# One transformer layer on one core: a reordered entry with products that nothing reads, row sums with one product, and half of the last output projection in the banks of the scores

## The chip, the core and the metric

The kernel runs on one core of one Trainium2 chip. TensorE (PE) does the matrix products, VectorE (DVE), ScalarE (ACT) and GpSimd (POOL) the rest, and SyncE (SP) issues most of the DMAs. The metric is the device time in microseconds, the median over runs; before the change it is 1199.61 us (three runs, 1198.49 to 1199.99).

## The reference

One decoder layer on a sequence of 1024 tokens of width 1024, in float32: an entry LayerNorm, two groups of attention heads side by side (sliding window with sinks, and stick-breaking), one output projection over both, LayerNorm, SwiGLU, LayerNorm.

```
h = layer_norm(x, ln_in_g, ln_in_b)
proj = h @ w_in          # q, k, v of both groups
sb_out, swa_out = stick_breaking_attention(...), sliding_window_attention(...)
merged = concatenate([rms_norm(sb_out, sb_norm_g), rms_norm(swa_out, swa_norm_g)])
h = layer_norm(ALPHA * h + merged @ w_out, ln1_g, ln1_b)
h = layer_norm(ALPHA * h + (silu(h @ gate) * (h @ up)) @ w_down, ln2_g, ln2_b)
```

## The kernel before, in words

Float32 accuracy comes from splitting each operand into a high and a low part and adding three products (hi*hi, hi*lo, lo*hi, helper `mm3`, L169 to L175). A scheduler places the instructions of each engine in a fixed order; each engine then runs its own in that order, and a wait at one instruction holds all behind it. The stages, in order of time:

- **Entry (0 to about 50 us).** The gain and bias rows `g_in` and `b_in` are spread over the partitions by four products with a row of ones (L269) and copied by ACT (L270). The eight token tiles x0 to x7 are normed (`entry`, L303 to L314): statistics on DVE (L141), the power of the variance on POOL (L135), the scaling on DVE alone for x0 and x1 (L151, L154) and on ACT, DVE and POOL for the others (L161, L162, L164). PE turns each tile in two groups of four transposes (L117) in the banks `tr`; ACT takes the high part (`xh`, L121), PE subtracts it with the negated identity `negi` (L124), and ACT takes the low part (`xl`, L125). The normed tile goes to `h_dram` on ACT's queue. Weight strips (`w_sw`, 512 KB each) arrive in two buffers `raw`; ACT casts the high part (L108), POOL subtracts (L109).
- **Projections and attention (to about 490 us).** `xmul` makes k, v and q of a strip (24 products of 256 columns per chunk of 256 tokens, bank `pp`). For v the result is copied from PSUM by DVE (`vr`, L343) and turned by PE (`pv`, L346). Scores lie in the banks `z`, transposed weights in `tra` or `trp`, outputs in `av`. A helper (`merge`) interleaves the attention of one head pair with the projection of the next; in the last pair it interleaves the output projection of the window group (`c1_steps`).
- **Output projection** (`out_load`, `out_proj`, L505 to L535): once in `c1_steps` for the window group (adds to h, result to `acc_dram`), once after the attention for the stick-breaking group, in the order of chunks 0, 2, 1, 3. `out_load` brings a chunk `m` of 512 features by 256 tokens, splits it (L510, L511) and squares it in place (L512). `out_proj` makes the row sum of squares of a token tile with four products against ones (`pr`, L522), then two halves of 512 columns (`pc`, twelve products each); DVE scales and adds each half to `acc` (L533). `pr` and both `pc` lie in the two buffers of bank `pp`. After the second one each tile is normed, written to `h1_dram` and turned for the FFN (`put_b`, banks `tr` and `av`).
- **FFN (from about 556 us).** Gate and up by a scheme with seven products of half size, then the down projection and the last norm. The change does not touch it.

Of the kernel before, what the change touches and what calls it, by code (L numbers as in the profile page):

```python
# [21 lines left out]
P = 128  # L22
# [27 lines left out]
class Ordered:  # L50
# [13 lines left out]
    def matmul(self, *a, **k):  # L64
        self._queue(self.eng.matmul(*a, **k))

    def transpose(self, *a, **k):
        self._queue(self.eng.transpose(*a, **k))

    def dma_start(self, *a, **k):  # L70
        self._queue(self.eng.dma_start(*a, **k))
# [3 lines left out]
def layer(ctx: ExitStack, tc: tile.TileContext, x, ln_in, w_sw, w_sb, norm_g,  # L75
          sinks, rel_bias, onehot, w_out, ln1, w_gu, w_down, ln2, out):
    nc = tc.nc
    pe, act, dve, pool = nc.tensor, nc.scalar, nc.vector, nc.gpsimd
# [28 lines left out]
    def split_w(raw, hi, lo):  # L107
        act.copy(hi, raw)  # L108
        pool.tensor_tensor(out=lo, in0=raw, in1=_f(hi), op=ALU.subtract)  # L109

# [26 lines left out]
    def ln_stats(xt, n=2, eps=LN_EPS):  # L137
        bst = st.tile([P, n, 6], F32, tag=f"bst{n}", name="bst")
        w = D // n
        for i in range(n):  # L140
            dve.bn_stats(out=bst[:, i, :], in_=xt[:, i * w:(i + 1) * w])  # L141
        mv = st.tile([P, 2], F32, tag="mv", name="mv")
        dve.bn_aggr(out=mv, in_=bst)  # L143
        rstd = st.tile([P, 1], F32, tag="rstd", name="rstd")
        rpow(rstd, mv[:, 1:2], 1.0, eps)
        return mv[:, 0:1], rstd

    def ln_apply(dst, xt, g, b, fast=False, eps=LN_EPS):
        mu, rstd = ln_stats(xt, 2, eps)
        if fast:  # L150
            dve.scalar_tensor_tensor(out=dst, in0=xt, scalar=mu, in1=g, op0=ALU.subtract, op1=ALU.mult)  # L151
            for i in range(2):
                h = slice(i * 512, i * 512 + 512)
                dve.scalar_tensor_tensor(out=dst[:, h], in0=dst[:, h], scalar=rstd, in1=b[:, h],  # L154
                                         op0=ALU.mult, op1=ALU.add)
            return
        nmu = st.tile([P, 1], F32, tag="nmu", name="nmu")
        dve.tensor_scalar(out=nmu, in0=mu, scalar1=-1.0, scalar2=None, op0=ALU.mult)
        for i in range(2):
            h = slice(i * 512, i * 512 + 512)  # L160
# [40 lines left out]
    def strip(i, ahead=2):  # L201
        while len(loaded) < min(len(strips), i + ahead):
# [3 lines left out]
            split_w(raw, hi, lo)  # L206
# [59 lines left out]
    for i, dst in enumerate((g_in, b_in)):  # L266
        for h in (slice(0, 512), slice(512, D)):
            ps = bps.tile([P, 512], F32, tag=("pp", "av")[i], name="bc")
            pe.matmul(ps, row1, rows[i][:, h], start=True, stop=True)  # L269
            act.copy(dst[:, h], ps)  # L270
# [32 lines left out]
    def entry(t):  # L303
        xt = xts.pop(t)
        ln_apply(xt, xt, g_in, b_in, t < 2)
# [8 lines left out]
        act.dma_start(h_dram[t], xt)  # L314
# [24 lines left out]
    def put_v(ps, c0, nc_, vts):  # L339
# [3 lines left out]
        dve.tensor_copy(vr.rearrange("p a b -> p (a b)"), ps)  # L343
# [161 lines left out]
    def out_load(g, c):  # L505
# [7 lines left out]
        return mh, ml, m  # L513

    def out_proj(c, m, wo, acc):
        mh, ml, ss = m
        for i in range(2):
# [3 lines left out]
            for k in range(4):  # L521
                pe.matmul(pr, ss[:, k, tok], ones, start=(k == 0), stop=(k == 3))  # L522
# [6 lines left out]
            for d in range(2):  # L529
                ds = slice(d * 512, d * 512 + 512)  # L530
                ps = bps.tile([P, 512], F32, tag="pp", name="pc")
# [22 lines left out]
    entry(0)  # L554
    entry(1)
    for c in range(4):
# [4 lines left out]
        if c < 3:  # L561
            entry(2 * c + 2)
            entry(2 * c + 3)
        swa_q(0, 0, q0, c, 1)
        swa_q(0, 1, q0, c, 1)
        if c > 0:
            next(att0)
            next(att0)
# [28 lines left out]

    def c1_steps():
        ms = [out_load(1, 0), out_load(1, 1)]
        for c in range(4):  # L600
# [3 lines left out]
            if c < 2:  # L604
                ms.append(out_load(1, c + 2))

# [40 lines left out]
    ms = {c: out_load(0, c) for c in order[:2]}  # L647
    hs = {}
    d0, d1 = slice(0, 512), slice(512, D)
    for n, c in enumerate(order):  # L650
        if n in (1, 2):
            ms[order[n + 1]] = out_load(0, order[n + 1])
        for t, h in out_proj(c, ms[c], wo, load_acc(c, acc_dram)):
# [215 lines left out]
    with tc.tile_pool(name="dn", bufs=4, reuse_waits="tile") as dn:  # L869
# [8 lines left out]
        def one(t):  # L878
# [6 lines left out]
            mu, rstd = ln_stats(h[t], 4)  # L885
# [104 lines left out]
```

## Time and profile before

| | |
|---|---|
| median of three runs | 1199.61 us |
| the profiled execution: its own time, its span | 1199.59 us, 1197.9 us |
| mean granted TensorE clock | 0.986 |
| busy share PE, DVE, ACT, POOL | 96%, 70%, 49%, 49% |
| stretches of 30 us in which PE is busy under 27 us | 0 to 60, 360 to 390, 450 to 480, 540 to 570, the end |

The span is the time from the first to the last instruction of the profiled execution; 1.7 us of its own time lie around it. PE is busy nearly always, so a reader looks at what PE is given to do, and at the stretches in which it waits or runs at the lower clock level.

### The profile page before, as it was taken

The page shows a single profiled execution, that of the slowest core. Times are in us where ns is not written, and L with a number is a line of the kernel's source. Part 1 is how long each engine was busy: PE and PEld are TensorE (multiplying, and loading weights), DVE is VectorE, ACT ScalarE, POOL GpSimd, SP SyncE. Part 2 cuts the span into 40 slices and gives each one's busy share as a digit, 9 for nine tenths or more (in the row PEclk, how much of TensorE's full clock was granted, in tenths as well). Part 3 has the DMA queues.
Part 4 walks back from the last instruction along what each step waited for, and adds up shares of the span by engine and source line. Part 5 has one row for each costly group of instructions (what it writes and reads, how often), then busy time and mean ns, then how long its engine had stood idle before and what let it go on. Part 6 is the DMA issues. An engine that isn't in the chain of part 4 may idle for free. (4 is left out here: it accounts for less than half of the span.)

```text
span 1197.9 us, 17900 instructions
## 1 busy us (share of the span) xinstructions
PE 1154.2 (96%) x6394; PEld 997.9 (83%) x6394; DVE 837.7 (70%) x1291; ACT 581.3 (49%) x1255; POOL 591.8 (49%) x572
## 2 busy tenths in 40 slices
PE   6899999999998998998999999999999999999997
PEld 4888998999998887876888888888888888888885
DVE  8776687887889895866765555564565448899735
ACT  5666577767677654346333232223233224456531
POOL 5623435566646463214777657665577521000584
PEclk9999999999999998999999999999999999999999
DMA  7403012110105525243333223422232339853431
GB/s 249 167 15 93 27 28 76 28 62 25 48 19 182 196 93 191 83 141 141 114 132 114 89 79 115 131 90 96 97 114 97 106 111 388 328 185 106 131 123 70
DMA packets 59913, 140.17 MB, mean 117 GB/s; under 512 B 7046, under 2 KB 18863, under 8 KB 59825
## 3 DMA queue, kind: packets, MB, share of 16 engines
q1 hardware_dynamic: 45264, 110.19, 28.6%
q10 hardware_dynamic: 14560, 28.85, 6.2%
q8 instruction: 50, 0.82, 0.3%
q14 instruction: 39, 0.31, 0.1%
HBM read 95.23 MB, written 41.17 MB: 114 GB/s over the span
## 5 line engine op out<-in xcount | busy, mean ns | idle before, releaser
L109 POOL TENSOR_TENSOR w<-s,w 128x512 fp32r<-128x512 f32 x88 | 124.0, 1412 | 121.4 <-ACT w L108 121.4
L174 PE MATMUL pp<-xh,whi 128*128 128x256 f32 x544 | 157.3, 290 | 1.4 <-DVE q L337 1.4
L174 PE MATMUL pp<-xh,wlo 128*128 128x256 f32 x544 | 157.0, 289 | 0.0
L174 PE MATMUL pp<-xl,whi 128*128 128x256 f32 x544 | 156.6, 288 | 0.0
L108 ACT CAST w<-s 128x512 fp32r<-128x512 f32 x88 | 54.6, 622 | 201.9 <-PE pgu L730 119.9
L803 PE MATMUL pd<-bhl,ahl 128*128 128x512 f32 x612 | 139.2, 389 | 0.0
L803 PEld LDWEIGHTS pd<-bhl,ahl 128*128 128x128 f32 x612 | 114.8, 188 | 24.2 <-DVE bhl L795 0.4
L762 DVE TENSOR_TENSOR t<-t,pgu 128x512 f32<-128x512 f32 x88 | 60.0, 682 | 98.7 <-PE pgu L730 95.6
L454 POOL TENSOR_TENSOR s<-s,s 128x127 f32<-128x127 f32 (+2 forms) x96 | 91.5, 956 | 51.8 <-DVE s L450 25.0
L174 PEld LDWEIGHTS pp<-xh,whi 128*128 128x128 f32 x544 | 105.5, 194 | 2.5 <-DVE q L337 1.7
L174 PEld LDWEIGHTS pp<-xl,whi 128*128 128x128 f32 x544 | 105.2, 193 | 1.5 <-ACT xl L125 0.3
L174 PEld LDWEIGHTS pp<-xh,wlo 128*128 128x128 f32 x544 | 105.2, 193 | 1.3
L795 POOL TENSOR_TENSOR ahl<-ar,ahl 128x512 fp32r<-128x512 f32 x12 | 16.2, 1353 | 134.8 <-ACT ahl L794 134.7
L450 DVE TENSOR_TENSOR_SCAN s<-s,brk 128x128 f32<-128x128 f32 (+1 forms) x64 | 69.4, 1089 | 12.0 <-ACT s L441 11.2
L794 ACT CAST ahl<-ar 128x512 fp32r<-128x512 f32 x63 | 39.1, 622 | 77.1 <-PE pd L803 50.2
L112 ACT CAST at<-tra 128x256 fp32r<-128x256 f32 (+1 forms) x160 | 55.2, 355 | 36.4 <-DVE at L113 19.0
L395 POOL TENSOR_TENSOR L<-L,rd 128x512 f32<-128x512 f32 (+1 forms) x32 | 30.9, 988 | 81.7 <-DVE rd L393 80.0
L109 POOL TENSOR_TENSOR w<-gr,w 128x512 fp32r<-128x512 f32 x44 | 62.2, 1424 | 8.1 <-ACT w L108 8.1
L113 DVE TENSOR_TENSOR at<-tra,at 128x256 fp32r<-128x256 f32 (+1 forms) x160 | 58.8, 382 | 8.8 <-ACT at L112 7.5
L730 PE MATMUL pgu<-B11h,w 128*128 128x512 f32 x176 | 59.1, 397 | 2.1 <-ACT w L108 1.5
L441 ACT ACTIVATE s<-z 128x128 f32<-128x128 f32 (+2 forms) x96 | 47.6, 498 | 23.9 <-PE z L440 15.7
L730 PE MATMUL pgu<-T4h,w 128*128 128x512 f32 x176 | 57.9, 390 | 0.4 <-DVE t L762 0.4
(234 smaller groups left out, 3315.6 us busy)
## 6 DMA issues: line engine op xcount, KB each, us to landing
ar<-a_dram SPq DMA_DIRECT2D x73, 256.0 KB, 3.1
a_dram<-act ACTq DMA_DIRECT2D x33, 512.0 KB, 2.6
gr<-in_w_gu SPq DMA_DIRECT2D x24, 512.0 KB, 3.4
ur<-in_w_gu SPq DMA_DIRECT2D x23, 512.0 KB, 3.5
bq<-in_w_down SPq DMA_DIRECT2D x44, 256.0 KB, 5.2
raw<-in_w_sb SPq DMA_DIRECT2D x12, 512.0 KB, 3.6
h_dram<-x ACTq DMA_DIRECT2D x8, 512.0 KB, 5.2
m<-o_dram SPq DMA_DIRECT2D x32, 128.0 KB, 2.8
```

What stands on the lines that cost most here:

```text
L108: act.copy(hi, raw)
L109: pool.tensor_tensor(out=lo, in0=raw, in1=_f(hi), op=ALU.subtract)
L112: act.copy(hi, ps)
L113: dve.tensor_tensor(out=lo, in0=ps, in1=_f(hi), op=ALU.subtract)
L174: pe.matmul(ps, a, b, start=(i == 0), stop=(i == n - 1))
L441: act.activation(s2[:, 0:w], ps, AF.Sigmoid, scale=-SCALE)
L450: dve.tensor_tensor_scan(s2[:, 0:w][:, ::-1], s2[:, 0:w][:, ::-1], brk[:, 512 - w:][:, ::-1] if last else zero.broadcast_to([P, w]), 1.0 i ...
L454: pool.tensor_tensor(out=s1[:, 0:m], in0=s1[:, 0:m], in1=s2[:, 1:m + 1], op=ALU.mult)
L730: pe.matmul(ps, a, b, start=(start and n == 0), stop=(stop and n == 11), skip_group_check=True)
L762: add = lambda out, x: dve.tensor_tensor(out=out, in0=x, in1=ps, op=ALU.add)
L794: act.copy(w[:, 0], src)
L803: pe.matmul(pd[t], x, y, start=(first and k == 0 and n == 0), stop=(end and k == KF - 1 and n == 2), skip_group_check=True)
```

## The change

Six edits. (1) `entry` is cut in two: `norm` (norming, store) and `turn_in` (transposes). The statistics of tile t come on DVE after the last step of tile t-1; x2 to x7 are normed before the q products of a chunk and turned after them; x0 and x1 are stored on SP's queue. (2) `warm` adds 3, 12 and 6 products of `negi` with itself before, between and after the transposes of x0 and x1, in a bank of the scores; nothing reads them. (3) The first two strips are split in halves, after the copies of `g_in` and `b_in` on ACT. (4) The copy `vr` moves from DVE to ACT, twelve times. (5) `out_load` adds the four blocks of squares on POOL (two additions, eight chunks), and `pr` is one product in place of four, for sixteen tiles. (6) The chunk 0 of the last projection is loaded and split during `c1_steps`, and the first half of a tile's `pc` lies in a bank of the scores (`z`) for three of four chunks.

```diff
@@ Ordered: every operation of an engine can be recorded; a wait-free order can be added
-    def matmul(self, *a, **k):
-        self._queue(self.eng.matmul(*a, **k))
-
-    def transpose(self, *a, **k):
-        self._queue(self.eng.transpose(*a, **k))
-
-    def dma_start(self, *a, **k):
-        self._queue(self.eng.dma_start(*a, **k))
+    def __getattr__(self, name):
+        f = getattr(self.eng, name)
+        if not self.on:
+            self.last = None
+            return f
+
+        def call(*a, **k):
+            self._queue(f(*a, **k))
+        return call
+
+    def after(self, ins, before):
+        self.tc.add_manual_dep(
+            ins.ins, before.ins.name,
+            mybir.DependencyInfo(mybir.DependencyClass.NoSync, mybir.DependencyReason.DATA),
+            reason="traced order")
...
-    pe, act, dve, pool = nc.tensor, nc.scalar, nc.vector, nc.gpsimd
+    pe, act, dve, pool = Ordered(tc, nc.tensor), nc.scalar, nc.vector, nc.gpsimd
...
@@ strip: the first two weight strips are split in halves, the first after the copies of g_in and b_in
-            split_w(raw, hi, lo)
+            for k in (slice(0, 4), slice(4, KT)) if i_ < 2 else (slice(0, KT),):
+                ins = split_w(raw[:, k], hi[:, k], lo[:, k])
+                if i_ == 0:
+                    pe.after(ins, copied)
...
-            act.copy(dst[:, h], ps)
+            copied = act.copy(dst[:, h], ps)
...
@@ entry(t) becomes norm(t) and turn_in(t)
-    def entry(t):
+    ended = []
+
+    def warm(n):
+
+        ps = bps.tile([P, P], F32, tag="z", bufs=ZB, name="warm")
+        for i in range(n):
+            pe.matmul(ps, negi, negi, start=True, stop=True)
+
+    def norm(t):
+        xt = xts[t]
+        first, last = ln_apply(xt, xt, g_in, b_in, t < 2)
+        if t > 0:
+            for ins in first:
+                pe.after(ins, ended[t - 1])
+        ended.append(last)
+        (act if t > 1 else sp).dma_start(h_dram[t], xt)
+
+    def turn_in(t):
         xt = xts.pop(t)
-        ln_apply(xt, xt, g_in, b_in, t < 2)
...
-        act.dma_start(h_dram[t], xt)
...
-        dve.tensor_copy(vr.rearrange("p a b -> p (a b)"), ps)
+        act.copy(vr.rearrange("p a b -> p (a b)"), ps)
...
@@ out_load, out_proj: squares summed on GpSimd, one product for the row sum, a bank per half
-        return mh, ml, m
-
-    def out_proj(c, m, wo, acc):
+        pool.tensor_tensor(out=m[:, 0:2], in0=m[:, 0:2], in1=m[:, 2:4], op=ALU.add)
+        pool.tensor_tensor(out=m[:, 0], in0=m[:, 0], in1=m[:, 1], op=ALU.add)
+        return mh, ml, m[:, 0]
+
+    def out_proj(c, m, wo, acc, banks=("pp", "pp")):
...
-            for k in range(4):
-                pe.matmul(pr, ss[:, k, tok], ones, start=(k == 0), stop=(k == 3))
+            pe.matmul(pr, ss[:, tok], ones, start=True, stop=True)
...
-                ps = bps.tile([P, 512], F32, tag="pp", name="pc")
+                ps = bps.tile([P, 512], F32, tag=banks[d], name="pc")
...
-    entry(0)
-    entry(1)
+    norm(0)
+    norm(1)
+    pe.on, pe.last = True, None
+    warm(3)
+    turn_in(0)
+    warm(12)
+    turn_in(1)
+    warm(6)
+    pe.on = False
...
-        if c < 3:
-            entry(2 * c + 2)
-            entry(2 * c + 3)
+        for t in (2 * c + 2, 2 * c + 3)[:NT - 2 - 2 * c]:
+            norm(t)
         swa_q(0, 0, q0, c, 1)
         swa_q(0, 1, q0, c, 1)
+        for t in (2 * c + 2, 2 * c + 3)[:NT - 2 - 2 * c]:
+            turn_in(t)
...
@@ c1_steps and the last projection
             if c < 2:
                 ms.append(out_load(1, c + 2))
+            elif c == 2:
+                m0.append(out_load(0, 0))
...
-    ms = {c: out_load(0, c) for c in order[:2]}
+    ms = {0: m0[0], order[1]: out_load(0, order[1])}
...
-        for t, h in out_proj(c, ms[c], wo, load_acc(c, acc_dram)):
+        for t, h in out_proj(c, ms[c], wo, load_acc(c, acc_dram), ("z" if n < 3 else "pp", "pp")):
```

The helpers `ln_stats`, `ln_apply` and `split_w` return the instructions that `after` is called with.

The scheduler's order on ACT at the entry, after the table load; before the change (`whi` and `whu` are the high parts of weight strips, `x_158` and `x_163` are x0 and x1, `x_199` and `x_201` x2 and x3, `xh_134` and `xl_135` hold x0 and x1):

```order
L270 COPY g_in<-bc 128x512 x2
L270 COPY b_in<-bc 128x512
L108 CAST whi<-raw 128x1024 x2
L270 COPY b_in<-bc 128x512
L121 CAST xh_134<-trx 128x4x128
L125 CAST xl_135<-trx 128x4x128
L314 DMA h_dram_84<-x_158 128x1024
L121 CAST xh_134<-trx 128x4x128
L314 DMA h_dram_85<-x_163 128x1024
L121 CAST xh_134<-trx 128x4x128
L108 CAST whi<-raw 128x1024
L161 ACTIVATE x_199<-x_199,nmu 128x512 x2
```

After the change (x0 to x3 are `x_158`, `x_163`, `x_203`, `x_205`):

```order
L282 COPY g_in<-bc 128x512 x2
L282 COPY b_in<-bc 128x512 x2
L115 CAST whi<-raw 128x512 x4
L129 CAST xh_134<-trx 128x4x128 x2
L133 CAST xl_135<-trx 128x4x128 x2
L115 CAST whi<-raw 128x1024
L303 COPY es<-pe__233 8x384
L115 CAST whu<-raw 128x1024
L304 DMA e_dram<-es 8x384
L129 CAST xh_134<-trx 128x4x128
L169 ACTIVATE x_203<-x_203,nmu 128x512 x2
L129 CAST xh_134<-trx 128x4x128
```

The second half of `b_in` now comes ahead of the casts of the first strips, the two stores are gone from ACT, and the casts of the third and fourth strip (`whi` 128x1024, `whu`) stand ahead of the high part of x1.

The scheduler's order on PE at the start of the last projection (`wo` is the weight of the window group, `woh` and `wol` that of the stick-breaking group); before the change:

```order
L174 MATMUL pc<-wo_5317,whi 128x512 x2
L174 MATMUL pc<-wo_5317,wlo 128x512
L487 MATMUL av<-at,v 128x256
L488 MATMUL av<-at,v 128x256
L487 MATMUL av<-at,v 128x256
L488 MATMUL av<-at,v 128x256
L522 MATMUL pr<-ones,m 128x1 x4
L174 MATMUL pc<-woh,whi 128x512
L174 MATMUL pc<-wol,whi 128x512
L174 MATMUL pc<-woh,wlo 128x512
L174 MATMUL pc<-woh,whi 128x512
```

After the change:

```order
L183 MATMUL pc<-wo_5345,whi 128x512 x2
L183 MATMUL pc<-wo_5345,wlo 128x512
L550 MATMUL pr<-ones,m 128x1
L514 MATMUL av<-at,v 128x256
L466 MATMUL z<-kd,q 128x512
L467 MATMUL z<-kl,q 128x512
L515 MATMUL av<-at,v 128x256
L514 MATMUL av<-at,v 128x256
L515 MATMUL av<-at,v 128x256
L183 MATMUL pc<-woh,whi 128x512
L183 MATMUL pc<-wol,whi 128x512
L183 MATMUL pc<-woh,wlo 128x512
```

The first twelve products of the last projection stood behind the last output products of their stretch and behind `pr`; now they follow the last scores (`z`) directly, with the last token tile of the window group and the last transposes and outputs of the attention still to come, and their `pr` comes later.

## Rows read from the trace of the kernel before

**Rows 1.** The page's first part: busy us, share and instructions by engine.

```profile
PE 1154.2 (96%) x6394; PEld 997.9 (83%) x6394; DVE 837.7 (70%) x1291; ACT 581.3 (49%) x1255; POOL 591.8 (49%) x572
```

**Rows 2.** PE's waits: us in total, times, longest.

```profile
PE pv L346 <- DVE vr L343: 4.8, 4, 1.9
...
PE pr L522 <- DVE res L533: 2.7, 1, 2.7
...
PE av L487 <- ACT at L112: 1.5, 1, 1.5
...
PE pr L522 <- ACT m L512: 1.1, 1, 1.1
PE av L488 <- DMA res<-acc_dram: 0.9, 1, 0.9
```

**Rows 3.** Windows: length, busy us by engine, granted clock, DMA share, GB/s.

```profile
80.00:90.00 10.00, 8.05 (x51) 7.33 (x50) 6.92 (x14) 6.02 (x16) 3.51 (x4) 0.83 0.05 16
195.00:200.00 5.00, 4.77 (x28) 4.77 (x29) 2.99 (x7) 4.36 (x11) 3.90 (x7) 0.66 0.55 159
380.00:395.00 15.00, 12.26 (x64) 10.66 (x65) 13.58 (x22) 12.12 (x24) 5.99 (x7) 0.77 0.69 226
465.00:480.00 15.00, 11.46 (x48) 9.26 (x47) 7.34 (x13) 7.79 (x14) 1.91 (x2) 0.77 0.56 200
520.00:525.00 5.00, 5.00 (x20) 4.05 (x19) 4.52 (x9) 1.26 (x2) 1.83 (x2) 0.66 0.29 109
420.00:460.00 40.00, 40.00 (x233) 34.73 (x233) 35.19 (x55) 22.11 (x52) 27.88 (x36) 1.00 0.30 102
```

**Rows 4.** Timeline of PE in the entry: start, us, instruction, idle before.

```profile
17.73 1.97 PE L117 MATMUL trx<-ident,x 128*128 128x128 f32 x8 [4.01 <-DVE x L154]
...
24.15 0.56 PE L174 MATMUL pp<-xl,whi 128*128 128x256 f32 x1
24.51 0.41 PE L174 MATMUL pp<-xh,wlo 128*128 128x256 f32 x1
24.72 0.41 PE L174 MATMUL pp<-xh,whi 128*128 128x256 f32 x1
...
47.69 0.39 PE L174 MATMUL pp<-xh,whi 128*128 128x256 f32 x1 [1.44 <-DVE q L337]
...
48.04 0.28 PE L174 MATMUL pp<-xh,wlo 128*128 128x256 f32 x1
48.15 0.28 PE L174 MATMUL pp<-xh,whi 128*128 128x256 f32 x1
```

**Rows 5.** Timeline of PE around a row sum.

```profile
381.81 0.95 PE L522 MATMUL pr<-ones,m 128*128 128x1 f32 x8
382.62 0.37 PE L487 MATMUL av<-at,v 128*128 128x256 f32 x1
```

**Rows 6.** POOL's groups from 370 to 480 us: busy, mean ns, idle before.

```profile
L454 POOL TENSOR_TENSOR s<-s,s 128x511 f32<-128x511 f32 x5 | 5.5, 1091 | 0.4
```

**Rows 7.** Timeline of DVE in the entry.

```profile
8.93 1.27 DVE L151 SCALAR_TENSOR_TENSOR x<-x,mv,g_in 128x1024 f32<-128x1024 f32 x1
...
11.07 3.32 DVE L151 SCALAR_TENSOR_TENSOR x<-x,mv,g_in 128x1024 f32<-128x1024 f32 x1
```

**Rows 8.** Timeline of POOL in the entry.

```profile
10.54 2.76 POOL L109 TENSOR_TENSOR wlo<-raw,whi 128x1024 fp32r<-128x1024 f32 x1 [2.10 <-ACT whi L108]
...
43.52 6.04 POOL L164 TENSOR_TENSOR x<-x,b_in 128x512 f32<-128x512 f32 x4
```

**Rows 9.** Timeline of ACT at the end of the attention.

```profile
465.76 1.04 ACT L510 CAST whi<-m 128x1024 fp32r<-128x1024 f32 x1 [6.22 <-DMA m<-o_dram]
466.71 0.36 ACT L112 CAST at<-tra 128x256 fp32r<-128x256 f32 x1
```

**Rows 10.** Timeline of DVE in the last projection.

```profile
518.33 1.41 DVE L533 SCALAR_TENSOR_TENSOR res<-pc,r,res 128x512 f32<-128x512 f32 x2 [4.74 <-DMA res<-acc_dram]
```

**Rows 11.** Timeline of ACT in the entry.

```profile
11.59 0.58 ACT L270 COPY b_in<-bc 128x512 f32<-128x512 f32 x1
```

**Rows 12.** The tile raw in the first 60 us: DMA times.

```profile
DMA to landing us min/median/max: 3.6/5.0/6.8
```

More of the change, by code (lines that the diff above doesn't have):

```diff
@@ L107, in split_w @@
     def split_w(raw, hi, lo):
-        act.copy(hi, raw)
+        ins = act.copy(hi, raw)
         pool.tensor_tensor(out=lo, in0=raw, in1=_f(hi), op=ALU.subtract)
+        return ins
     def split_ps(ps, hi, lo):
@@ L138, in ln_stats @@
         bst = st.tile([P, n, 6], F32, tag=f"bst{n}", name="bst")
-        w = D // n
+        w, first = D // n, []
         for i in range(n):
-            dve.bn_stats(out=bst[:, i, :], in_=xt[:, i * w:(i + 1) * w])
+            first.append(dve.bn_stats(out=bst[:, i, :], in_=xt[:, i * w:(i + 1) * w]))
         mv = st.tile([P, 2], F32, tag="mv", name="mv")
@@ L145, in ln_stats @@
         rpow(rstd, mv[:, 1:2], 1.0, eps)
-        return mv[:, 0:1], rstd
+        return mv[:, 0:1], rstd, first
     def ln_apply(dst, xt, g, b, fast=False, eps=LN_EPS):
-        mu, rstd = ln_stats(xt, 2, eps)
+        mu, rstd, first = ln_stats(xt, 2, eps)
         if fast:
@@ L153, in ln_apply @@
                 h = slice(i * 512, i * 512 + 512)
-                dve.scalar_tensor_tensor(out=dst[:, h], in0=dst[:, h], scalar=rstd, in1=b[:, h],
-                                         op0=ALU.mult, op1=ALU.add)
-            return
+                last = dve.scalar_tensor_tensor(out=dst[:, h], in0=dst[:, h], scalar=rstd, in1=b[:, h],
+                                                op0=ALU.mult, op1=ALU.add)
+            return first, last
         nmu = st.tile([P, 1], F32, tag="nmu", name="nmu")
-        dve.tensor_scalar(out=nmu, in0=mu, scalar1=-1.0, scalar2=None, op0=ALU.mult)
+        last = dve.tensor_scalar(out=nmu, in0=mu, scalar1=-1.0, scalar2=None, op0=ALU.mult)
         for i in range(2):
@@ L164, in ln_apply @@
             pool.tensor_tensor(out=dst[:, h], in0=dst[:, h], in1=b[:, h], op=ALU.add)
+        return first, last
     def bc_load(dst, src):
@@ L596, in load_acc @@
         return res
+    m0 = []
     def c1_steps():
@@ L884, in one @@
                 return
-            mu, rstd = ln_stats(h[t], 4)
+            mu, rstd, _ = ln_stats(h[t], 4)
             for x in (d0, d1):
```

## The prediction, made before the changed kernel was run

> **What bounds the kernel now.** I read the page's busy shares first [rows 1]: PE is busy 1154.2 of 1197.9 us, so 44 us are idle, and next to nothing can be won on another engine alone. The list of PE's waits comes second [rows 2]: the reader is to see that no wait dominates; the longest sums are 4.8 us for the copy `vr` and 2.7 us before a row sum, and three waits of 0.9 to 1.5 us stand together at the end of the attention. Third come windows with the granted clock [rows 3], because a wait costs twice: after it PE works for some microseconds at the lower level. In 465 to 480 PE is idle 15 - 11.46 = 3.5 us, and a clock of 0.77 costs another 0.23 x 15 = 3.45 us; in 380 to 395 the two are 2.7 and 3.45 us, in 195 to 200 1.7 us of clock, in 520 to 525 1.7 us, in 80 to 90 1.95 and 1.7 us. The middle of the attention is the contrast: from 420 to 460 PE is busy all the time at clock 1.00, and there a product left out is time won.
>
> The entry must be read from the timeline [rows 4], since its clock column says 1.00 although the products tell otherwise: at 24.5 us a product of 256 columns follows the last after 0.21 us (256 / 0.21 is 1.2 GHz), at 48 us after 0.11 to 0.12 us (2.4 GHz). PE had waited 4.01 us for x0's second half just before.
>
> **The change part by part.** All sums are made against the profiled execution's own 1199.59 us; the median of the runs, 1199.61, is the same for this purpose.
>
> *Row sums.* Four products against ones are eight instructions here, and the next product on PE starts 382.62 - 381.81 = 0.81 us after the first [rows 5]. One product leaves two of the eight, 0.20 us. Sixteen tiles save 16 x 0.61 = 9.7 us of PE. Eight tiles lie in `c1_steps`, where PE is dense, and count fully; the other eight lie in the last projection, where DVE and DMAs also end waits, and I count 60% of their 4.9 us: -7.8 us. In place of the products POOL gets two additions for each of eight chunks, about 1.1 us by a row of the same width [rows 6] and half of that for the half as wide one, 8 x 1.65 = 13.2 us in all, and POOL is busy 27.9 of 40 us there [rows 3]. They are hidden unless `pr` is the next thing PE needs, or unless they hold DVE up. Bounds: -9.7, and +13.2 - 9.7 = +3.5 if every addition delayed DVE by its length and DVE set the end.
>
> On that last point a row speaks against the change. The scaling of x0 takes 1.27 us; that of x1, the same instruction, takes 3.32 us from 11.07 [rows 7], and meanwhile POOL works on a weight strip from 10.54 to 13.30 [rows 8]. The wait is 13.30 - 11.07 = 2.2 us, which is 3.32 less 1.27 to within 0.2. The Trainium skill, "SBUF — State Buffer", section "Who interferes with whom", says that a VectorE instruction with two SBUF inputs contends with a GpSimd instruction that reads SBUF, and that the later one blocks until the other is done. The trace agrees at this place; by that rule each added POOL addition can block DVE, which is the rival "lock" below.
>
> *Chunk 0 loaded early.* Before, ACT stands 6.22 us at the cast of `m`, and the cast of attention weights that PE needs is behind it [rows 9]. Those are the three waits of 1.5, 1.1 and 0.9 us, and the low clock from 470 on. Now the first chunk's load, cast and square lie among the attention's work, four loads and not eight are left at that place, and twelve products of the last projection fill PE there. The load of chunk 2 still needs the attention's third chunk, and its cast still stands ahead of the last attention casts. Bounds 0 and -(3.5 + 3.45) = -7; I take -5.
>
> *Half of `pc` in the scores' banks.* Before, `pr` waits 2.7 us for DVE, which itself waits 4.74 us for the load of `acc` [rows 10]. This load is late in both kernels, because SP's queue has four stores ahead of it that wait for finished norms. What changes is that PE can go on: with `pc` in `z` and `pp` the next `pr` and twelve products, 0.2 + 12 x 0.21 = 2.7 us, need no bank of DVE's. The wait of 2.7 us goes, and with it the 1.7 us of clock. Late next is the second half of that tile, in `pp`. Bounds 0 and -4.4; I take -3.
>
> *The copy `vr` on ACT.* It is a matter of the queue, not of the copy's length: before, the copy waits behind scans and additions, and four `pv` wait 4.8 us for it. ACT is less busy, but the copy now stands behind softmax exponentials and casts that wait themselves. Bounds: all of it gone with the clock it costs, -(4.8 + 1.7 + 3.45) = -9.95; or each of the eight wide ones stalls as the worst one does, 1.9 us, with a clock loss behind it of up to 3.45 us: 8 x 5.35 - 9.95 = +33. Nearer to the first, since the work in between on PE is about as long as before: -2.
>
> *Entry.* Both halves of `b_in` are copied before the weight casts, so its second half comes not at 11.59 but one cast of 1.05 sooner, at 10.6 [rows 11]; x0 is finished one step of 0.7 later (half of the 1.27 of [rows 7]), at about 11.3, and turned 6 us earlier. x1 isn't: its variance power on POOL now comes behind four half strips, 4 x 1.3 us (half of 2.76 or a little less, [rows 8]) from 11.2, so x1 ends near 18 as before. Then ACT holds x1's high part back: ahead of it is the cast of the fourth strip, whose load is issued when POOL is done with the second (about 16.5) and lands 3.6 us later at best, 20.1, so the cast ends at 21.1 and x1's two high parts follow at 21.7 and about 23.6. The first low-part product comes at 24.8, not earlier than before (24.15) [rows 4]. What is won lies behind it: the q products of chunk 0 no longer stand behind transposes of tiles that POOL hasn't finished, and POOL's last entry addition ends at about 46, not 49.6 [rows 8], as it starts on x2 1.5 us sooner and the six tiles have less between them. By hand I get chunk 1's first product at about 43.4 against 47.69 us; 1.2 us of that is work moved behind it, so -3. Bounds: -8 when the wait and clock of 80 to 90 us (3.65) and more go as well, +3.2 when the strip's load takes 6.8 us and not 3.6 [rows 12]. The stores on SP put the later x loads at 18 us and not 17.5, which x5 to x7 can bear.
>
> *The products that nothing reads* are 21 of 128 columns, 0.1 us each at the low level: three ahead of the spreading of the gains (0.3 us), twelve in a wait for x1, six ahead of the low-part products (0.65 us, in the sum above). I count no gain for the clock: between the twelve and the first projection product PE still waits some 3 us for ACT.
>
> *The new order.* Nearly every row between 50 and 550 us moves a little. The old order has 4.8 + 2.7 + 1.5 + 1.1 + 0.9 = 11 us of such waits [rows 2]; that the new one makes or takes half as much in other places bounds the price by -5.5 and +5.5. I take half the upper end, +2.8.
>
> Sum: -7.8 - 5 - 3 - 2 - 3 + 2.8 = -18.0, so 1199.6 - 18.0 = 1181.6 us.
>
> **The rivals.**
> - *All waits go.* Row sums in full, chunk 0 and the banks at their bounds and the copy at half of its own: -9.7 - 7 - 4.4 - 5 - 3 = -29, 1170.5 us; if the clock also rises before chunk 0's k products, 24 x (0.21 - 0.12) = 2.2 us more, 1168. For it: these waits have one cause each. Against it: the fixed order of five engines changes with them.
> - *The freed time isn't on the path.* DVE is busy 35.2 of 40 us from 420 to 460 and the loads of `acc` come no earlier, so PE waits where it worked. Then the entry and half of the window group's share stay: 1199.6 - 3 - 2.5 = 1194. Against it: DVE waits for PE in the last projection more than the reverse.
> - *Lock.* The additions of POOL block DVE: of the 13.2 us what falls on a busy DVE is given back, 35.2 of 40 us in the one stretch and 7.3 of 15 in the other [rows 3], some 0.7 on the mean: 9.2 us, 1181.6 + 9.2 = 1191.
> - *Nothing that can be measured.* The new waits eat the gain: 1199.
> - *Slower: `vr` behind ACT's queue.* Place: the eight wide v copies between 120 and 385 us. Price: 1.9 us and 3.45 us of low clock each. With all eight, 1181.6 + 2 + 33 = 1217; it decides from the fifth stalled copy on, as the other terms hold 16 us and n copies cost n x 5.35 - 9.95. For it: the copy now shares a queue with casts that wait for DVE. Against it: PE's order has about as many other products directly ahead of `pv` as before.
>
> **How the numbers follow.** No change is what lies within 0.2%, 2.4 us, about what a measurement of this kernel can tell. Forecast (1174 to 1189) 0.58; all waits go 0.12; not on the path 0.14, one part in ten of it within 0.2%; lock 0.06; nothing 0.04; slower 0.06. Faster: 0.58 + 0.12 + 0.126 + 0.06 = 0.89; same 0.05; slower 0.06. The range goes from 1168 (the second clock level of the first rival) to 1197; some 0.05 lies below it and 0.11 above.
>
> **What would show it.** Row sums: `pr` with a quarter of the instructions and the dense stretch before 460 some 5 us shorter. Chunk 0: no wait of ACT for `m` over 3 us, and clock over 0.9 in the 15 us that answer to 465 to 480. Banks: no wait of PE over 1 us before a `pr`. Copy: `pv` waits under 4.8 us in all. Entry: chunk 1's first product before 45 us, POOL's last entry addition before 47. It is wrong if one of those stretches is as long as before, or if `pv` waits 10 us for ACT. From the gate products on, at 556 us, nothing should differ but a shift.

## The result and the profile after

The changed kernel takes 1191.0 us (median of 4 runs, 1188.7 to 1192.6) against 1199.8 before; the ratio is 0.992, 95% interval 0.9906 to 0.9935. So 8.8 us were won where 18.0 were forecast. The sign was right, the time lies in the range, but 2 us above the likeliest case's own range. The profiled execution took 1192.59 us (span 1190.8), the slowest of the four.

Where it came from, by a few events of PE's timeline, each from the one profiled execution of its kernel (start in us; the v transposes are the products `pv`, two at a time for each of chunks 0 to 3 at first, four at a time, "wide", from 180 us on):

| kernel | chunk 1's v | first wide v | last v | last pc | median, us | ratio to before |
|---|---|---|---|---|---|---|
| before | 55.6 | 183.1 | 381.3 | 543.9 | 1199.8 | |
| after | 61.7 | 189.2 | 384.5 | 536.0 | 1191.0 | 0.9906 to 0.9935 |
| e1 old entry, rest new | 55.8 | 179.6 | 374.3 | 533.5 | 1187.9 | 0.9877 to 0.9907 |
| e2 new entry alone | 61.9 | 188.5 | 388.0 | 550.5 | 1205.8 | 1.0032 to 1.0062 |
| e3 scalings held | 64.0 | 190.0 | 385.0 | 536.4 | 1193.7 | 0.9934 to 0.9958 |
| e4 vr on DVE | 61.6 | 187.9 | 387.2 | 543.7 | 1197.0 | 0.9971 to 0.9996 |
| e5 scalings held in two parts | 59.9 | 188.5 | 382.0 | 540.0 | 1195.4 | 0.9944 to 0.9972 |
| e6 four products | 61.6 | 189.0 | 384.2 | 539.9 | 1195.1 | 0.995 to 0.9975 |
| e7 chunk 0 late | 61.4 | 188.9 | 384.0 | 533.7 | 1192.4 | 0.9925 to 0.995 |
| e8 old entry, vr on DVE | 57.2 | 185.0 | 382.0 | 535.2 | 1191.2 | 0.9919 to 0.9944 |
| e9 fourth strip later | 56.0 | 187.5 | 383.2 | 534.3 | 1188.7 | 0.9879 to 0.9912 |
| e10 old first tiles | 57.4 | 182.9 | 378.1 | 529.9 | 1187.7 | 0.988 to 0.9908 |
| e11 one kind of bank | 60.6 | 187.7 | 382.9 | 544.3 | 1199.1 | 0.9983 to 1.0004 |
| e12 no unread products | 60.4 | 184.0 | 377.1 | 534.7 | 1190.0 | 0.9899 to 0.9926 |

PE's order differs between some of them, so that up to 2 us of work more or less lies ahead of an event. Between chunk 1's v and the first wide v the kernels take 123.6 (e12) to 131.5 us (e9), so what is won at the one does not arrive unchanged at the other. From the last v to the last `pc` the change takes 536.0 - 384.5 = 151.5 us and not 162.6: 11 us won. The entry loses 6.1 us by chunk 1's v. The attention in between takes 195.3 us and not 198.3. From the gate products on there is a shift, as forecast (548.61 to the span's end 642.2 us, before 641.1).

The page of the changed kernel, engines as in [rows 1], and its waits of PE, as in [rows 2]:

```profile
PE 1147.4 (96%) x6319; PEld 989.4 (83%) x6319; DVE 836.0 (70%) x1279; ACT 584.5 (49%) x1269; POOL 622.0 (52%) x590
```

```profile
PE trx L132 <- ACT xh L129: 4.7, 2, 4.3
...
PE pv L373 <- ACT vr L370: 1.9, 1, 1.9
...
PE pr L550 <- POOL m L541: 1.2, 1, 1.2
...
PE pr L550 <- DVE res L561: 0.2, 1, 0.2
```

Of the 4.8 us for `vr` 1.9 are left, and of the 2.7 us before a row sum 0.2; on top stands one wait of 4.3 us, and it is in the entry. Windows, as in [rows 3]: the first two are the entry, the last answers to the end of the attention.

```profile
30.00:40.00 10.00, 4.95 (x40) 4.32 (x38) 10.00 (x15) 2.79 (x6) 8.56 (x6) 0.82 0.33 135
40.00:47.00 7.00, 5.94 (x27) 5.71 (x28) 5.87 (x11) 4.79 (x12) 5.71 (x6) 0.53 0.44 169
465.00:480.00 15.00, 15.00 (x85) 12.95 (x84) 7.79 (x17) 6.04 (x13) 4.04 (x5) 1.00 0.77 277
```

The end of the attention is full at clock 1.00, where 11.46 us and 0.77 stood. The entry is the reverse: PE idles 5 of 10 us, then works at 0.53. Its chain is read backwards through four timelines of the changed kernel (start, us, instruction, idle before). PE, to set beside [rows 4]:

```profile
25.18 1.38 PE L71 MATMUL warm<-negi 128*128 128x128 f32 x6
26.35 0.52 PE L183 MATMUL pp<-xl,whi 128*128 128x256 f32 x1
...
41.06 0.80 PE L132 MATMUL trx<-xh,negi 128*128 128x512 f32 x1 [4.25 <-ACT xh L129]
...
41.89 0.41 PE L183 MATMUL pp<-xl,whi 128*128 128x256 f32 x1
42.10 0.41 PE L183 MATMUL pp<-xh,wlo 128*128 128x256 f32 x1
...
53.21 0.36 PE L183 MATMUL pp<-xh,whi 128*128 128x256 f32 x1
```

ACT, and under it DVE:

```profile
35.43 0.33 ACTq L330 DMA_DIRECT2D h_dram<-x  x1
35.80 0.37 ACT L370 COPY vr<-pp 128x256 f32<-128x256 f32 x1 [3.21 <-POOL x L172]
39.65 0.37 ACT L355 CAST kd<-pp 64x256 fp32r<-64x256 f32 x1 [3.48 <-DVE kl L357]
...
40.42 0.58 ACT L129 CAST xh<-trx 128x512 fp32r<-128x512 f32 x1
```

```profile
23.55 2.28 DVE L170 SCALAR_TENSOR_TENSOR x<-x,rstd,g_in 128x512 f32<-128x512 f32 x1 [0.80 <-ACT x L169]
...
25.88 0.69 DVE L170 SCALAR_TENSOR_TENSOR x<-x,rstd,g_in 128x512 f32<-128x512 f32 x1
...
29.98 1.28 DVE L149 BATCH_NORM_STATS2 bst<-x 128x6 f32<-128x512 f32 x2
31.18 6.44 DVE L170 SCALAR_TENSOR_TENSOR x<-x,rstd,g_in 128x512 f32<-128x512 f32 x5
...
37.66 1.62 DVE L170 SCALAR_TENSOR_TENSOR x<-x,rstd,g_in 128x512 f32<-128x512 f32 x1
39.21 0.41 DVE L357 TENSOR_TENSOR kl<-pp,kd 64x256 fp32r<-64x256 f32 x1
```

POOL, as in [rows 8]:

```profile
22.91 2.37 POOL L116 TENSOR_TENSOR wlu<-raw,whu 128x1024 fp32r<-128x1024 f32 x1
25.91 3.05 POOL L172 TENSOR_TENSOR x<-x,b_in 128x512 f32<-128x512 f32 x2 [0.63 <-DVE x L170]
28.92 1.06 POOL L143 TENSOR_TENSOR rstd<-mv,mhalf 128x1 f32<-128x1 f32 x2
...
31.99 8.42 POOL L172 TENSOR_TENSOR x<-x,b_in 128x512 f32<-128x512 f32 x5 [1.29 <-DVE x L170]
...
43.94 6.34 POOL L172 TENSOR_TENSOR x<-x,b_in 128x512 f32<-128x512 f32 x4 [1.29 <-DVE x L170]
```

PE waits for a high part that ACT casts at 40.42. ACT stood 3.48 us at the cast of the second head's k, because DVE had not done the first head's low part `kl`; that one stood behind six scalings in a row, 1.29 us each beside POOL's additions, where one alone takes 0.69. They began only at 31.2. Two things lie ahead of them. On POOL x3's power comes at 28.9, behind x2's additions, and these behind the fourth strip's subtraction `wlu`, which also holds up DVE's first scaling of x2. On DVE itself the scheduler has put the statistics of x4, x5 and x6 first, the last from 29.98, so DVE is busy until 31.2 and never stands still for the power. In the kernel before six scalings in all stand ahead of `kl` (x2 to x4; now eight, x2 to x5), and the last five run from 24.25, seven us sooner, under PE's k products, and `wlu` comes at 34. Its DVE and its POOL:

```profile
24.25 6.47 DVE L162 SCALAR_TENSOR_TENSOR x<-x,rstd,g_in 128x512 f32<-128x512 f32 x5
...
33.09 0.42 DVE L330 TENSOR_TENSOR kl<-pp,kd 64x256 fp32r<-64x256 f32 x1 [1.18 <-ACT kd L329]
```

```profile
25.36 4.80 POOL L164 TENSOR_TENSOR x<-x,b_in 128x512 f32<-128x512 f32 x3
34.32 2.36 POOL L109 TENSOR_TENSOR wlu<-raw,whu 128x1024 fp32r<-128x1024 f32 x1
```

### The profile page after: what moved, and what is told of

It reads as the page before. It is cut to its first block, busy times and chain, and to the rows that moved or that the text cites. A ratio compares the mean times of both kernels' runs of the same rounds, so it can differ in the third digit from the quotient of the medians.

```text
span 1190.8 us, 17761 instructions
## 1 busy us (share of the span) xinstructions
PE 1147.4 (96%) x6319; PEld 989.4 (83%) x6319; DVE 836.0 (70%) x1279; ACT 584.5 (49%) x1269; POOL 622.0 (52%) x590
## 5 line engine op out<-in xcount | busy, mean ns | idle before, releaser
L481 POOL TENSOR_TENSOR s<-s,s 128x127 f32<-128x127 f32 (+2 forms) x96 | 94.6, 990 | 42.6 <-DVE s L477 20.8
L477 DVE TENSOR_TENSOR_SCAN s<-s,brk 128x128 f32<-128x128 f32 (+1 forms) x64 | 72.8, 1143 | 8.8 <-ACT s L468 8.2
L770 PE MATMUL pgu<-T3h,w 128*128 128x512 f32 x176 | 57.9, 390 | 1.0 <-ACT w L115 1.0
```

The costliest lines, as they stand in the source:

```text
L477: dve.tensor_tensor_scan(s2[:, 0:w][:, ::-1], s2[:, 0:w][:, ::-1], brk[:, 512 - w:][:, ::-1] if last else zero.broadcast_to([P, w]), 1.0 i ...
L481: pool.tensor_tensor(out=s1[:, 0:m], in0=s1[:, 0:m], in1=s2[:, 1:m + 1], op=ALU.mult)
L770: pe.matmul(ps, a, b, start=(start and n == 0), stop=(stop and n == 11), skip_group_check=True)
```

## The experiments

Each was timed in five rounds against the kernel before. The first four ask where the entry's loss sits.

**e1_old_entry.** The functions `norm`, `turn_in` and `warm`, and the halved strips, go back to:

```diff
-    norm(0)
-    norm(1)
-    pe.on, pe.last = True, None
-    warm(3)
...
+    entry(0)
+    entry(1)
...
+        if c < 3:
+            entry(2 * c + 2)
+            entry(2 * c + 3)
```

> The changed kernel with the entry of the kernel before: no written order on PE, no unread products, strips cast whole, each tile normalised and turned in one go; the row sums, the early load of chunk 0, the banks and the copy vr on ACT stay. Theory Q (the new entry costs about 6 us, because in it chunk 0's low k parts stand behind six scalings on DVE that take turns with POOL's additions, and ACT's cast and PE behind them): 1199.8 - 7 - 6 = about 1185 us, ratio to the kernel before 0.987 or 0.988, and the first transposes of v of chunk 1 near 55.6 us as in the kernel before, not 61.7. Rival N (the entry's delay is a loan that the attention pays back anyway): 1191, ratio 0.992 to 0.993, though the same transposes come 6 us sooner.

1187.9 us: the entry's 6 us are back at chunk 1 (55.8), and half of it, 3.1 us, at the end (the ranges of the two kernels' runs just touch). Its last stage takes 159.2 us, not 151.5.

**e2_entry_only.** The other half: of the change only the entry.

It is the edits of e4, e6, e7 and e11 (their diffs are below) together.

> The kernel before with the new entry alone: row sums of four products, chunk 0 loaded late, both halves of pc in pp, the copy vr on DVE. Theory Q: it loses the 6 us of the entry and wins nothing elsewhere: 1199.8 + 6 = about 1206 us, ratio 1.004 to 1.006; the first transposes of v of chunk 1 come at 60 us or later, and PE waits 4 us or more for xh of x2 as in the changed kernel. Rival N: 1200, ratio 0.999 to 1.001. By the forecast of the entry alone it would be 1196.6, ratio 0.997.

1205.8 us, 6 us slower than before. With e1 this settles that the new entry loses; rival N, that the attention pays the delay back, falls.

**e3_hold.** Two orders added, for the scalings (`held[0]` is chunk 0's second `kl`) and the stores (`copies[0]` is its `vr`):

```diff
+            if behind:
+                pe.after(ins, behind)
...
+behind=held[0] if t > 3 else None)
...
+        if t > 1:
+            pe.after(ins, copies[0])
```

> The changed kernel with two orders added by hand and nothing else: DVE scales x4 to x7 only behind chunk 0's second low k part, and ACT issues the stores of x2 to x7 only behind chunk 0's copy vr. Theory Q: PE's wait of 4.25 us for xh at 41 us and that of 1.86 us for vr at 36 us shrink to under 1.5 us together, the 23 products behind them run at the upper level (2.2 us), and the first transposes of v of chunk 1 come near 55 us, not 61.7: 1191 - 6 = 1185 us, ratio 0.987. Rival W (the written order on PE and the unread products of the first two tiles cost it): the wait may go but chunk 1 comes no earlier than 60 us, and the time stays at 1191, ratio 0.992.

1193.7 us: missed. The wait for `xh` is gone, and the wait comes back one station on. Its waits of PE, and its DVE:

```profile
PE pp L185 <- DVE v L121: 5.4, 1, 5.4
```

```profile
37.95 11.50 DVE L170 SCALAR_TENSOR_TENSOR x<-x,rstd,g_in 128x512 f32<-128x512 f32 x8
49.48 0.29 DVE L121 TENSOR_TENSOR v<-pv,v 128x128 fp32r<-128x128 f32 x1
```

The held scalings fall into one block of eight, 1.44 us each, and chunk 0's low v part is behind it.

**e5_hold_split.** The same with x6 and x7 held behind chunk 0's last q part, `lasts[1]`:

```diff
-behind=held[0] if t > 3 else None)
+behind=lasts[1] if t > 5 else held[0] if t > 3 else None)
```

> As e3_hold, but x6 and x7 are scaled only behind the last low q part of chunk 0, and x4 and x5 behind chunk 0's second low k part as there. In e3_hold the wait for xh went, and PE then waited 5.4 us for chunk 0's low v part, which stood behind one block of eight scalings (11.5 us on DVE). Theory Q: with four scalings in that block the low v part ends near 44.5 us and not 49.8, PE's wait there falls under 1 us, chunk 1's first transposes of v come near 57 us: 1193.7 - 6 = about 1187 us, ratio 0.989 to 0.990, that of the kernel with the old entry. Rival M (the entry is bound by DVE's and POOL's work together, so the wait only moves on again): a wait of 4 us or more at another place before 65 us, and 1191 us or more, ratio 0.992 or above.

1195.4 us: missed by the time, though the 5.4 us went, no wait of PE from 30 to 66 us is over 1.6 us (rival M wanted one of 4), and chunk 1 came at 59.9, and the last v 2.5 us sooner than in the changed kernel. All of that and more was lost behind it: from the last v to the last `pc` 158.0 us, where PE's order is that of e1 and e12, instruction for instruction, and not the changed kernel's.

**e9_strip4_later.** The root of the chain instead of its end: `wlu` (`lows[5]`) behind x3's second addition (`adds[3]`):

```diff
             norm(t)
+            if t == 3:
+                pe.after(lows[5], adds[3])
```

> The changed kernel with one order added by hand: POOL takes the fourth strip's low part (2.37 us from 22.91 in the changed kernel) only behind the additions of x2 and x3. Theory P (this subtraction, pulled ahead by the new entry, is the root: it blocks DVE's first scaling of x2 for 2.28 us where the second takes 0.69, holds POOL's additions back to 25.9 and so x3's power to 28.9 and the scalings to 31.2, and these then stand ahead of chunk 0's low k part): the scalings of x2 take under 1.4 us each, the first low k part of chunk 0 ends by 35 us and not at 39.6, PE's wait for xh near 41 us falls under 1.5 us, chunk 1's first transposes of v come by 58 us: 1191 - 4 to - 6 = about 1186 us, ratio 0.987 to 0.989. Rival M (DVE and POOL have too much to do before 60 us in any order, so the wait moves on): another wait of 3 us or more before 60 us, chunk 1 not before 60 us, and 1191 us or more.

The mechanism came as expected. Its DVE:

```profile
23.54 0.75 DVE L172 SCALAR_TENSOR_TENSOR x<-x,rstd,g_in 128x512 f32<-128x512 f32 x1 [1.00 <-ACT x L171]
...
27.93 4.81 DVE L172 SCALAR_TENSOR_TENSOR x<-x,rstd,g_in 128x512 f32<-128x512 f32 x4 [1.10 <-POOL rstd L145]
...
34.35 0.41 DVE L359 TENSOR_TENSOR kl<-pp,kd 64x256 fp32r<-64x256 f32 x1
```

2.28 us became 0.75, `kl` came 5 us and chunk 1's v 5.7 us sooner. The added order redrew DVE's as well: only the statistics of x4 stand ahead of the scalings of x3 and x4, DVE now does wait for the power (1.10 us), and x5 is scaled behind `kl`. But 1188.7 us is 2.3 us less, not 4 to 6, and the intervals overlap: the first wide v comes only 1.7 us sooner. The rest went between 97 and 187 us, 90.1 us here, 85.2 in e10 for the same work in another order of PE. Windows of e9, then of e10:

```profile
96.00:110.00 14.00, 11.47 (x79) 10.04 (x79) 9.27 (x24) 10.78 (x33) 6.56 (x6) 0.95 0.44 138
110.00:125.00 15.00, 15.00 (x113) 14.53 (x113) 10.88 (x23) 6.81 (x21) 4.29 (x3) 0.93 0.16 45
```

```profile
96.00:110.00 14.00, 13.01 (x104) 12.29 (x103) 11.31 (x27) 10.52 (x33) 6.97 (x5) 1.00 0.51 143
110.00:125.00 15.00, 15.00 (x123) 14.57 (x121) 11.29 (x24) 9.98 (x29) 5.11 (x6) 1.00 0.16 45
```

In the first window PE idles 1.5 us more (its longest wait is 1.8 us for POOL's normalised scores), and the clock is below 1.00 in both, which is 0.05 x 14 + 0.07 x 15 = 1.75 us; the other 1.7 of the 5.0 us lie behind 125 us.

**e10_old_first_tiles.** No unread products, no written order on PE, whole strips; the later tiles stay as in the change.

```diff
-            for k in (slice(0, 4), slice(4, KT)) if i_ < 2 else (slice(0, KT),):
-                ins = split_w(raw[:, k], hi[:, k], lo[:, k])
+            split_w(raw, hi, lo)
...
-    norm(0)
-    norm(1)
-    warm(3)
...
+    for t in (0, 1):
+        norm(t)
+        turn_in(t)
```

> The changed kernel with its first tiles as before: no unread products, no written order on PE, strips cast whole; the norms of later tiles still stand ahead of the q products and their transposes behind them. If the first tiles' part costs the 6 us: chunk 1's first transposes of v near 56 us and the time of e1_old_entry, 1188 us, ratio 0.989 to 0.990. If the order of the later tiles does (theory P, with the fourth strip's subtraction still ahead of x2's additions on POOL): chunk 1 at 60 us or later and 1191 us, ratio 0.992.

1187.7 us, chunk 1 at 57.4, the first wide v 6.3 us sooner. From there to the last `pc` PE's order is the changed kernel's, instruction for instruction, and takes 347.0 us in the one and 346.8 in the other. So the 6.3 us belong to the first tiles' part; theory P, which put them on the later tiles, is wrong in that: the subtraction still stands ahead of x2's additions here, yet x5's scalings come behind `kl`, which starts at 35.9.

**e12_no_unread.** Nothing else than:

```diff
-    warm(3)
...
-    warm(12)
...
-    warm(6)
```

> The changed kernel without the 21 products that nothing reads. They are the only edit, but PE's order in the attention and in the output projection comes out as in e1_old_entry and e5_hold_split. Theory P (the fourth strip's subtraction on POOL and the scalings behind it cost the entry, not the unread products): the subtraction still stands ahead of x2's additions, a scaling of x2 still takes over 2 us, and the first wide transposes of v come at 187 to 189 us, as in all kernels with the new first tiles. Theory O (the order of the output projection is worth some 7 us by itself): from the last transposes of v to the last product pc 157 to 160 us as in those two (159.2 and 158.0), not 151.5, so 1193 to 1196 us, ratio 0.994 to 0.997. Rival H (the unread products are what costs the entry): the first wide transposes of v by 184 us, and 1189 us or less.

1190.0 us: not to be told from the changed kernel, and below the 1193 expected by theory O. Of the three expectations, P's holds for the mechanism and fails for the place: the scaling of x2 is still blocked (2.63 us), yet the first wide v comes at 184.0, 5.2 us sooner. `kl` starts at 35.6, behind the scalings of x2 to x4 and not of x5, but chunk 1's v comes only 1.3 us sooner; the other 3.9 us lie between there and the first wide v, and why isn't shown. H is right on that event, not on its time; O is right on the stage (157.6 us). As the edit also redraws the orders of DVE and POOL, the products' own cost in the time isn't shown. At their place it is: the first low-part product comes at 26.35 with them and at 24.52 without, but chunk 0's v at 36.22 and 36.15, so that waits swallow the difference there. And they don't raise the clock sooner. With them, products follow one another after 0.12 us, not 0.21, from 29.73 on:

```profile
29.61 0.28 PE L183 MATMUL pp<-xl,whi 128*128 128x256 f32 x1
29.73 0.28 PE L183 MATMUL pp<-xh,wlo 128*128 128x256 f32 x1
```

Without them from 27.74 on, 2.0 us sooner, in a run of products that also starts 1.8 us sooner:

```profile
24.52 0.58 PE L183 MATMUL pp<-xl,whi 128*128 128x256 f32 x1 [0.91 <-ACT xl L133]
...
27.62 0.28 PE L183 MATMUL pp<-xh,whi 128*128 128x256 f32 x1
27.74 0.28 PE L183 MATMUL pp<-xl,whi 128*128 128x256 f32 x1
```

The other four take the remaining terms, one at a time.

**e4_vr_on_dve** and **e8_old_entry_vr_dve** put the copy back, with the new and with the old entry:

```diff
-        act.copy(vr.rearrange("p a b -> p (a b)"), ps)
+        dve.tensor_copy(vr.rearrange("p a b -> p (a b)"), ps)
```

> The changed kernel with the copy vr on DVE as in the kernel before. Theory Q: in the entry nothing is won, since the copy now stands behind the same six scalings on DVE as the low k parts, so PE's wait there is 6 us or more in one piece; in the attention the waits of pv for vr that the kernel before had (4.8 us in all) come back in part: 1191 + 2 = 1193 us, ratio 0.993 to 0.995. Rival V (the copy on ACT, behind a store that waits for POOL, is what costs the entry): 1191 - 2 to - 6, ratio 0.987 to 0.990.

> The kernel of e1_old_entry (old entry, rest of the change) with the copy vr back on DVE. By the forecast's term, 2 us: 1187.9 + 2 = 1190 us, ratio 0.991 to 0.993. If the 6 us that the same edit cost in the changed kernel lie in the attention: 1194 us, ratio 0.994 to 0.996. If they lay in the new entry alone (the copy behind the same scalings on DVE): 1188 us, ratio 0.989 to 0.990.

1197.0 and 1191.2 us: the copy on ACT is worth 6.0 and 3.3 us. From the first wide v to the last, the four kernels with it on DVE take 197.0 to 199.4 us (before, e2, e4, e8), the ten with it on ACT 193.1 to 195.7. Of e4's loss against the changed kernel 4.0 us lie there and 5.0 after the last v, where PE's order changed with it; it is 1.3 us ahead at the first wide v.

**e6_four_products** restores the four products and drops POOL's additions:

```diff
-        pool.tensor_tensor(out=m[:, 0:2], in0=m[:, 0:2], in1=m[:, 2:4], op=ALU.add)
-        pool.tensor_tensor(out=m[:, 0], in0=m[:, 0], in1=m[:, 1], op=ALU.add)
...
-            pe.matmul(pr, ss[:, tok], ones, start=True, stop=True)
+            for k in range(4):
+                pe.matmul(pr, ss[:, k, tok], ones, start=(k == 0), stop=(k == 3))
```

> The changed kernel with the row sums as before: four products against ones, no additions on POOL. By the forecast's term (half of the tiles in full, 60% of the others): 1191 + 8 = 1199 us, ratio 0.998 to 1.000. If every saved product counted: 1191 + 9.7 = 1200.7. Rival (the freed time is not on the path): the time from the first row sum to the last pc grows from 149.5 by under 3 us, and 1191 to 1194 us, ratio 0.992 to 0.995. Rival lock (POOL's additions hold DVE up): without them the time falls below 1191 us in spite of the products.

1195.1 us: one product is worth 4.1, half of the term. Part of the rest can be seen in the stretch of `c1_steps`, which was counted in full because PE was dense there: with one product PE is busy 3.1 us less of the same 76 us. A window of the changed kernel, then the same of e6:

```profile
384.00:460.00 76.00, 70.22 (x373) 57.98 (x374) 66.59 (x102) 48.54 (x109) 55.12 (x72) 0.98 0.47 161
```

```profile
384.00:460.00 76.00, 73.30 (x420) 61.81 (x419) 63.98 (x106) 49.25 (x111) 39.01 (x63) 1.00 0.48 161
```

POOL's additions take 20.4 us in all, not 13.2. Two rows of the changed kernel (busy, mean ns, idle before), and one that stands in the same view of the kernel before as [rows 6], with the additions' own width:

```profile
L540 POOL TENSOR_TENSOR m<-m 128x512 f32<-128x512 f32 x8 | 13.4, 1674 | 13.8 <-ACT m L539 13.8
L541 POOL TENSOR_TENSOR m<-m 128x256 f32<-128x256 f32 x8 | 7.0, 876 | 0.2
```

```profile
L454 POOL TENSOR_TENSOR s<-s,s 128x512 f32<-128x512 f32 x12 | 17.8, 1487 | 21.2 <-ACT s L442 13.1 <-DVE s L450 3.9 <-ACT s L441 2.7
```

[rows 6] is the row of 511 columns, at 1091 ns; by this one, 1487 ns, the sum would have been 8 x 2.23 = 17.8 us.

In e1 the first row sum is the next thing PE needs, and waits for them; its PE:

```profile
378.66 0.59 PE L532 MATMUL pr<-ones,m 128*128 128x1 f32 x2 [2.56 <-POOL m L523]
```

e5 and e12 share this order and this wait (2.6 us). The three take 157.6 to 159.2 us behind the last v, the changed kernel 151.5; some 2 us of it are products that lie ahead of that event there.

**e7_chunk0_late** takes out `m0`:

```diff
-            elif c == 2:
-                m0.append(out_load(0, 0))
...
-    ms = {0: m0[0], order[1]: out_load(0, order[1])}
+    ms = {c: out_load(0, c) for c in order[:2]}
```

> The changed kernel with chunk 0 of the last projection loaded after the attention, as before. By the forecast's term: 1191 + 5 = 1196 us, ratio 0.996 to 0.998, ACT's wait for a DMA of m of 5 us or more is back near 460 us, and the clock of the 15 us behind it falls below 0.9. Rival (other products fill the place, so that the early load only moved work): 1191 us, ratio 0.992 to 0.993.

1192.4 us, 1.4 more, with overlapping intervals: the rival holds. ACT's longest wait for `m` grows from 2.0 to 3.7 us, and PE is nearly full at that place all the same, in a window of e7:

```profile
460.00:475.00 15.00, 14.85 (x75) 12.34 (x75) 8.57 (x14) 8.25 (x15) 7.63 (x7) 1.00 0.80 282
```

Its last `pc` even comes 2.3 us sooner than the changed kernel's, but from there to the end of the span it takes 657.1 us and not 654.8.

**e11_one_bank** puts both halves of `pc` in `pp`:

```diff
-        for t, h in out_proj(c, ms[c], wo, load_acc(c, acc_dram), ("z" if n < 3 else "pp", "pp")):
+        for t, h in out_proj(c, ms[c], wo, load_acc(c, acc_dram)):
```

> The changed kernel with both halves of pc in the banks pp, as before. By the forecast's term: 1191 + 3 = 1194 us, ratio 0.994 to 0.996, and a wait of PE of 2 us or more before a row sum for DVE is back. Rival (other work of PE covers it now): 1191 us, ratio 0.992, no such wait.

1199.1 us, 8.1 more: undone alone, the banks cost nearly the whole gain. PE's wait before row sums and DVE's two longest waits there, in e11:

```profile
PE pr L550 <- DVE res L561: 5.2, 3, 2.8
```

```profile
DVE wlo L538 <- ACT whi L537: 6.7, 2, 5.6
DVE res L561 <- DMA res<-acc_dram: 4.8, 1, 4.8
```

A window of e11, then the same of the changed kernel:

```profile
475.00:490.00 15.00, 9.15 (x42) 6.89 (x42) 9.41 (x17) 3.98 (x7) 4.54 (x5) 0.93 0.40 141
```

```profile
475.00:490.00 15.00, 15.00 (x83) 12.90 (x82) 13.21 (x25) 5.02 (x9) 5.79 (x8) 1.00 0.45 155
```

The wait of [rows 10] is back, at 520 us: DVE waits 4.8 us for `acc`, and PE 2.8 us for DVE. That is the one the forecast priced. The larger loss is at another place, the window shown: chunk 0's products are there now, since it is loaded early, DVE stands 5.6 us at the low part of a later chunk (`wlo`, behind ACT's cast), has not emptied the two buffers of `pp`, and PE idles 5.9 us. In the kernel before chunk 0's products came later; so a part of the 8.1 is what the early chunk needs of the banks, and no run has both undone with the rest kept.

No run is the sum of these: undone singly they give 4.1 + 1.4 + 8.1 + 6.0, less 3.3 for the entry (e10), that is 16.3 and not 8.8 us; each edit redraws the orders of the others. The best kernels are e10 and e1, 3 us below the changed one (intervals that overlap a little).

## Why the prediction was right in sign and 9 us short

- **Entry, forecast -3, bounds -8 to +3.2: the step that failed.** It stands in the sentence that POOL "starts on x2 1.5 us sooner". POOL started at 25.91, 0.55 later than before, since the fourth strip's subtraction had moved ahead of x2, and ended its last addition at 50.28, not 46. I had followed the fourth strip on ACT and not on POOL, and had not followed `kl` in DVE's queue: it starts at 39.2, behind the scalings of x2 to x5, and at 33.1 to 35.9 in every kernel in which x5's come behind it (before, e1, e3, e5, e8, e9, e10, e12). Chunk 1's first product came at 53.2, not 43.4. The cost at chunk 1's v is 6.1 us against the kernel before (undone, 5.9 us come back in e1 and 4.3 in e10; at the first wide v 9.6 and 6.3). In the time it is 6.1 us when the entry is the only edit (e2), outside the bounds, and 3.1 and 3.3 when it is undone in the changed kernel (e1, e10), at their edge.
- **Row sums, -7.8.** Mechanism right, size 4.1. The step that was too large is counting the eight tiles of `c1_steps` in full: some 3 us of what was freed there is idle time of PE now (70.22 busy against 73.30). POOL's additions take 20.4 us, not 13.2, and `pr` waits for them (1.2 us in the changed kernel, 2.6 in e1). How the rest divides isn't shown.
- **Chunk 0 early, -5.** Mis-sized: 1.4, within the interval of nothing. The sign of success that I had named (end of the attention full, clock 1.00, ACT's longest wait for `m` 2.0 us) came true without it making the time.
- **Banks, -3, bounds 0 to -4.4.** Mechanism right, size 8.1 when undone alone. The wait that the term priced, 2.7 us in [rows 2], is 2.8 in e11; the 5.9 us of idling that come on top of it lie where chunk 0's products now are, a place that the term did not look at.
- **`vr` on ACT, -2.** Right in place and sign: 3 us in the attention, 3.3 to 6.0 in the time. The rival named for it did show itself once, not at the wide copies but in the entry (a store that waits for POOL ahead of the copy, 1.9 us).
- **Unread products.** No gain for the clock, as forecast. They are twice as long as forecast: the six ahead of the low-part products take 1.17 us (25.18 to 26.35), not 0.65, and the first low-part product comes at 26.35, not 24.8. Their place in the orders was not foreseen.
- **New order, +2.8 (±5.5).** No run shows the term by itself. That an order can be worth as much is shown: e1, e5 and e12, with one order of PE in the last stage, take 4 to 6 us longer there than the changed kernel.
- **Rivals.** "Lock" gave 1191, the measured time, for a wrong reason: taking the additions out (e6) costs time. Its mechanism acts in the entry: a scaling of x2 takes 2.28 us beside `wlu` and 0.69 alone. That agrees with the Trainium skill ("SBUF — State Buffer", "Who interferes with whom"), by which a VectorE instruction with two SBUF inputs contends with a GpSimd instruction that reads SBUF, and the one that comes later blocks. "Not on the path" (1194) holds for half of the row sums.

That the time still fell within the range is luck in part: undone singly, the banks and `vr` give 6 to 9 us more than their terms, and the row sums, chunk 0 and the entry some 13 less.

What stays open: which of the first tiles' edits (unread products, written order, halved strips) costs the entry's 6 us by itself, since each redraws DVE's and POOL's orders; and what sets the 123.6 to 131.5 us between chunk 1's v and the first wide v.

## What to carry to other kernels

When an entry is reordered, follow each moved tile through every queue that touches it, the slow helper's first: here one subtraction 11 us earlier on POOL, and two more scalings ahead of `kl` on DVE, came to lie where PE had no cover. A wait that is taken away at its end can move to the next instruction in the same queue (e3); taken away further up (e9) it brought chunk 1's v 5.7 us sooner, but the time by no more than 2.3 us. And with a fixed order of five engines, price an edit by undoing it in the new kernel as well as by the wait that it had in the old one, and look where the time goes: the banks cost 8.1 us when undone, of which their old wait is 2.8. Such a price includes what other edits need of this one, so the prices do not add up.

## What was not expected of the hardware

Scalings on DVE in turn with additions on POOL took 1.29 us each in the changed kernel and 1.44 in e3's block of eight, against 0.69 to 0.75 alone: while both engines work on the tiles in turn, DVE runs at about half its speed. And short idling can cost the clock too: in e9 1.5 us more of it than in e10, in waits of 1.8 us and less, went with a granted clock of 0.95 and 0.93 in the 29 us from 96 on, about as much time again.
